# Four edits to the order of work in a two-layer hybrid encoder: latents scaled on ScalarE, key and value units inside gates, norm sums and pooled product one step later

## Chip, cores and metric

One core of one Trainium2 chip. The metric is the device time of one execution in microseconds. The profile names the engines PE (TensorE), DVE (VectorE), ACT (ScalarE), POOL (GpSimd) and SP (SyncE, which issues most DMAs).

## What is computed

The input is 512 tokens by 1024 features, float32. Each of two layers does this:

```python
h = rms_norm(x, attn_norm_g[l])
proj = h @ w_in[l]
c_q, c_kv, k_rope, gq, gk, gv, pool_in, gate_logits = split_columns(proj, IN_SIZES)
o_mla = mla_branch(c_q, c_kv, k_rope, ...)    # c_q, c_kv: RMS-normed, then up-projected to 8 heads
o_gqa = gqa_branch(gq, gk, gv, ...)           # 8 query heads, 2 key/value heads
o_pool = pool_branch(pool_in, ...)            # centred means over 2/4/8/16 tokens minus the token, a 128x128 map per group
gates = sigmoid(gate_logits)                  # three gates of 1024 features
merged = (gates[0] * (o_mla @ w_branch_mla[l]) + gates[1] * (o_gqa @ w_branch_gqa[l])
          + gates[2] * (o_pool @ w_branch_pool[l]))
x = x + merged @ w_out[l]
hf = rms_norm(x, ffn_norm_g[l])
u = depthwise_conv(hf @ ffn_w_up[l], ...)
x = x + (silu(u[..., :2816]) * u[..., 2816:]) @ ffn_w_down[l]
```

## The kernel before

**Arithmetic.** Every matmul operand is split into a high half, rounded to fp32r, and a low half, the remainder, and a product is three matmuls: high by high, high by low, low by high (`mm3`). The high half is an ACT copy, the low half a subtraction on DVE or POOL. Weights come from HBM in pieces of up to 512 columns, two or three to one DMA slot (tile `raw`, three buffers, read by SP). `w_split` makes `wh` on ACT and `wl` on POOL or DVE, three pieces ahead of use (`LA = 3`, six buffers). The next read into a `raw` buffer waits until the last `wl` of that buffer has been made.

**Order.** The order of instructions on every engine is written out when the kernel is built. `Clock` is a planner: each matmul moves its clock on by the number of columns over 2370 us, and the work of the other engines is queued as chains of steps that are issued when the planner thinks that their inputs are there. What is issued earlier stands earlier in an engine's queue, and each engine works in order. So a wrong guess of the planner makes an engine wait at the head of its queue. `ps(tag)` takes a bank of PSUM: `acc`, `ST` and `AV` have two banks, `S` and `mi` one.

**Stages of a layer.**

1. The latents `c_q` and `c_kv` (384 columns, token-major, four blocks of 128 tokens, banks acc and ST).
2. Pool channels, feature-major, four tiles of eight k-steps (three matmuls of 512 columns each). Between two k-steps `norm_finish` may issue the matmul that finishes the norm's sums (`prt`); `rt` and `rbc`, the row factors, follow from it. `norm_finish` is issued as soon as the planner thinks that `prt` is ready, at the latest at g == 1, n == 6. With `rt`, ACT evacuates the latents (`lat_evac`) and takes sums of squares; POOL raises them to the power -1/2 (`ssc`); DVE scales the four blocks by them (`lat_norm`), two instructions to a block. Then `lat_turn` transposes the blocks in 32x32 squares on DVE, writes them to HBM (`dl`, four writes) and reads them back feature-major (`tf`, twelve reads), all on SP, and splits them on ACT and DVE (`cth`, `ctl`).
3. GQA queries (512 columns, eight key steps, banks AV, AV, mi, ST). DVE rotates them (`gq_rope`), which frees the banks.
4. GQA keys, values and the rotary key (288 columns, eight key steps, banks acc, acc, S, ST). After four of these steps stands `pool_product`: four tiles in the banks of the queries, from the pooled channels `mixed` (`mxh`, `mxl`).
5. GQA attention, with gate and branch tiles as filler between its matmuls. A gate tile is eight units of one k-step, a branch tile four. `EXTRA` and `_order` put the up-projections of the MLA latents among them: four query units (`q`), two units of two blocks of keys without position (`n`), and two of values (`v`). All take the acc banks. A query unit stands before every second unit of the following tiles, a key or value unit before every fourth (`gap`): so the first stands before a gate, in the place between two tiles, and the second before its k-step 4. A value unit's bank is freed by two copies (`vm`, ACT or DVE) and four remainders on DVE.
6. Gate tiles alone, until the first MLA head is turned, and then MLA attention with the remaining gates and branches as filler.
7. The output projection, the second norm, the gated FFN with its convolution.

Of the kernel before, what the change touches and what calls it, by code (L numbers as in the profile page):

```python
# [14 lines left out]
ALU = mybir.AluOpType  # L15
# [3 lines left out]
P = 128  # L19
# [11 lines left out]
WIDE = 528  # L31
NWIDE = 5
RAW = 3
EXTRA = (("q", 2, (2, 5)), ("n", 2, (6, 7)), ("v", 1, (2, 5)))

SOONER = {1: 3 * KC, 0: 6 * KC}
LAG = {2: 1, 1: 4, 0: 8}
PRO = 0.47
PRE_A = 16
PRE_B = 8  # L40
LA = 3
# [4 lines left out]
        "mla": (-6.2, -2.9, -1.0, 0.1, 0.64, 1.678, 1.82, 35.5)}  # L46

D_ROW, D_OUT, D_IN, D_LAT = 3.4, 3.2, 4.0, 6.0
REST = 0.4
W_BIAS = 2.54  # L50
C_BIAS = 0.2
# [13 lines left out]
def _order(br):  # L65


    r, lag = [], LAG[br]
    for m in range(KC + lag):
        r += [(k, pos.index(m)) for k, b, pos in EXTRA if b == br and m in pos]  # L70
        if m < KC:
            r.append(("g", m))
        if m >= lag:
            r.append(("b", m - lag))
    return r
# [5 lines left out]

def _widths():

    r = [384] * KC + [T] * 8 + [T] * KC + [288] * 4 + [T] + [288] * 4
    for br in (2, 1, 0):
        for k, _ in _order(br):
            r += WIDTHS[k]
    return r + [T] * (2 * KC) + [T] * (4 * FC) + [T] * (2 * FC)


# [34 lines left out]
class Clock:  # L125
# [37 lines left out]
    def done(self, *key):  # L163
        self.ready[key] = self.fin + self.SEM
# [90 lines left out]
def trunk(ctx: ExitStack, tc: tile.TileContext, x, w, prm, gb, cst, out):  # L255
# [213 lines left out]

    def norm_finish(gen, out, force=False):  # L470

        if gen not in parts or not (force or ck.has(("prt", gen))):
            return
        need(("prt", gen))
        s2 = ps("S")
        mm(s2[:, :16], C[:, C_GRP:C_GRP + P], parts.pop(gen), True, True)
        a, a4 = small("fac", [P, 16]), small("fac4", [P, 16])
        rt, rbc = out["rt"], out["rbc"] = small("rt", [P, 4]), slot("rbc")

        def mean():  # L480
            V.tensor_scalar(a, s2[:, :16], 1.0 / D, EPS, ALU.mult, ALU.add)
            free("S")

        def tokens():
            V.tensor_tensor(a4, a, C[:, C_SEL:C_SEL + 16], ALU.mult)
            V.tensor_reduce(rt, a4.rearrange("p (b g) -> p b g", g=4), AX.X, ALU.add)
            done("rt", gen)

        def rows():
            V.transpose(rbc[:, :T].rearrange("p (j r) -> p j r", r=32), bc(a.unsqueeze(2), [P, 16, 32]))  # L490
            done("rbc", gen)

        chain(mean, lambda: G.tensor_tensor(a, a, bc(mhalf, [P, 16]), ALU.pow), tokens, rows, after=0.3)
# [43 lines left out]
    def layer(l, sq, xsrc):  # L537
# [36 lines left out]

        def tok_major(banks, wd, between=None):
            for kc in range(KC):
                if between and kc == 4:
                    between()
                wh, wl = wnext()
                need(("H", G1, kc))  # L580
                if st["use"] == 1:
                    for n, (x_, w_) in enumerate(((HH, wh), (HL, wh), (HH, wl))):
                        for b in range(4):
                            mm(banks[b][:, :wd], x_[:, kc, b * P:b * P + P], w_[:, :wd], n == 0, False)
                    continue
                for b in range(4):
                    bs = slice(b * P, b * P + P)
                    mm3(banks[b][:, :wd], HH[:, kc, bs], HL[:, kc, bs], wh[:, :wd], wl[:, :wd],
                        kc == 0, kc == KC - 1)
# [37 lines left out]
            for c0, n in ((0, 256), (1, 128)):  # L627
                V.tensor_scalar(ssc[:, :, c0:c0 + 1], ssc[:, :, c0:c0 + 1], 1.0 / n, EPS, ALU.mult, ALU.add)

        def lat_norm():  # L630
            for b in range(4):
                V.tensor_scalar(mx[b][:, 0:256], mx[b][:, 0:256], ssc[:, b, 0:1], None, ALU.mult)
                V.tensor_scalar(mx[b][:, 256:384], mx[b][:, 256:384], ssc[:, b, 1:2], None, ALU.mult)
            done("lat", l)

        def latents():
            chain(*[([("rt", G1)], lambda b=b: lat_evac(b)) for b in range(4)], lat_mean,
                  *rsqrt_steps(ssc.rearrange("p a b -> p (a b)"), 8, ("ssc", l)), lat_norm)

        latents()  # L640

# [46 lines left out]
        for g in range(4):  # L688
            acc = ps(ptags[g])
            for n, _ in enumerate(feat_major(acc, G1)):  # L690
                norm_finish(G1, nrm, g == 1 and n == 6)
            chain(*pool_steps(g, acc, ptags[g]))


# [2 lines left out]
        def lat_turn():  # L697
            d = dp.tile([4, P, 384], F32, tag=f"dl{l}", name=f"dl{l}")
            trs, tos = [], []

            def turn_block(b):
                trs.append(slot("tr"))
                V.transpose(trs[b][:, :384], mx[b][:, :384])

            def put(b):
                SY.dma_start(d[b], trs[b][:, :384])
                ck.fin = ck.now + (D_OUT if b == 3 else 0.1)

            def get(j):
                to = slot("tf")  # L710
                src = d.rearrange("b (i f) (c t) -> c f (b i) t", i=4, t=32)
                for c in range(4):
                    SY.dma_start(to[32 * c:32 * c + 32, :T].rearrange("f (g t) -> f g t", t=32), src[4 * j + c])  # L713
                chain(*split(lat[j][0][:, :T], lat[j][1][:, :T], to[:, :T], col(PRM_CQ + j)),
                      lambda: done("latT", l, j), after=D_LAT)
                ck.fin = ck.now + 1.5

            steps = []
            for b in range(4):
                steps += [lambda b=b: turn_block(b), lambda b=b: put(b)]  # L720
            chain(*steps, *[lambda j=j: get(j) for j in (2, 0, 1)], after=0.1)

        chain(([("lat", l)], lat_turn))


        qtags = ("AV", "AV", "mi", "ST")
# [140 lines left out]
        def gates(br, okey, odst, mode):  # L867
# [44 lines left out]
                    merged[m] = (mh, ml)  # L912
                    chain(product, add, *split(mh[:, :T], ml[:, :T], XM[:, m, :]), fin)

            extra, tick, gap = None, 0, 2
            for k, m in _order(br):
                if k in mla_make:
                    extra, tick, gap = mla_make[k](m), 0, 2 if k == "q" else 4
                    continue
                work = branch(m) if k == "b" else gate(m)  # L920
                more = True
                while more:
                    if extra and tick % gap == 0:
                        if next(extra, END) is END:
                            extra = None
                        yield
                    tick += 1
                    more = next(work, END) is not END
                    yield
# [675 lines left out]
def _pack_weights(i):  # L1605
    res = []
    for l in range(L):
        cq, ckv, kr, gq, gk, gv, pool, gate = np.split(
            i["w_in"][l], np.cumsum([256, 128, 32, 512, 128, 128, 512]), axis=1)

        def rows(*parts):
            wm = np.concatenate(parts, axis=1)
            return [wm[kc * P:kc * P + P] for kc in range(KC)]

        res += rows(cq, ckv)
        for g in range(4):
            res += _cut(_blocks(pool[:, g * P:g * P + P], KC))
        res += rows(gq)
        res += rows(gk, gv, kr)
        res.insert(len(res) - 4, i["pool_w"][l].transpose(1, 0, 2).reshape(P, T))  # L1620
        uq, ukv = i["mla_w_uq"][l], i["mla_w_ukv"][l].reshape(P, 8, P)

        wb = (i["w_branch_mla"][l], i["w_branch_gqa"][l], i["w_branch_pool"][l])
        for br in (2, 1, 0):
            for k, m in _order(br):
                c = slice(m * P, m * P + P)
                if k == "g":
                    res += _cut(_blocks(gate[:, br * D:(br + 1) * D][:, c], KC))
                elif k == "b":
                    res += _cut(_blocks(wb[br][:, c], 4))  # L1630
                elif k == "q":
                    res += [uq[kc * P:kc * P + P, m * 384:m * 384 + 384] for kc in range(2)]
                else:
                    c = slice(0, 64) if k == "n" else slice(64, P)
                    res.append(ukv[:, 4 * m:4 * m + 4, c].reshape(P, 256))
        for m in range(KC):
            res += _cut(_blocks(i["w_out"][l][:, m * P:m * P + P], KC))
        up = i["ffn_w_up"][l]
        for c in range(FC):
            for o in (0, D_FF):  # L1640
                res += _cut(_blocks(up[:, o + c * P:o + c * P + P], KC))
        dn = i["ffn_w_down"][l]
        res += _cut(np.concatenate([_blocks(dn[:, m * P:m * P + P], FC) for m in range(KC)], axis=1))
    pieces, swidth = _stream()
    assert [a.shape[1] for a in res] == [wd for _, _, wd in pieces]
    slots = [[] for _ in swidth]
    for (sl, _, _), a in zip(pieces, res):
        slots[sl].append(a)
    return np.concatenate([np.concatenate(a, axis=1).reshape(-1) for a in slots])
# [76 lines left out]
```

## Time and profile before

| | |
|---|---|
| median of 3 executions | 1580.51 us (1580.4 to 1582.9) |
| the profiled execution | 1580.47 us, of which 1578.5 us is the span of the profile |
| mean granted TensorE clock | 0.999 |
| busy: PE, DVE, ACT, POOL | 1566.6, 952.9, 787.4, 1021.1 us |
| instructions | 20363 |

In a profile row "start, duration, engine, line, operation, output <- inputs" the text in brackets is the idle time of the engine just before the instruction and what ended it; "xN" merges N instructions. Most operations are issued by a few helpers, so the tile tells more than the line. Matmuls overlap, and the shown duration of one is longer than its distance to the next.

### The profile page before, as it was taken

The numbers are of one execution on the slowest core, as the hardware profiler recorded it, in microseconds if no ns is written. First come the engines' busy times: TensorE is split into PE (matmuls) and PEld (weight loads), VectorE is DVE, ScalarE is ACT, GpSimd is POOL, SyncE is SP. The second block draws the span as 40 slices with busy tenths as digits, with TensorE's granted clock in tenths as the row PEclk, the third lists the DMA queues.
The fourth block names the chain that finished last, engine by engine and source line by source line (L and its number), as shares of the span: only waits on it lengthen the run. The fifth ranks groups of instructions, "written<-read, shape, count | busy, mean of one in ns | idle before, by whom it ended". The sixth has DMA issues, their size and how long they took to land.

```text
span 1578.5 us, 20363 instructions
## 1 busy us (share of the span) xinstructions
PE 1566.6 (99%) x7098; PEld 1310.3 (83%) x7098; DVE 952.9 (60%) x1360; ACT 787.4 (50%) x1426; POOL 1021.1 (65%) x890
## 2 busy tenths in 40 slices
PE   9999999999999999999999999999999999999999
PEld 8888888888888888888898888888888888888888
DVE  6877967866267776721047788678652777777000
ACT  6367866663444444432244677576534444444221
POOL 3864986854667667654577649868547766676542
PEclk9999999999999999999999999999999999999999
DMA  5432234314333233333334322343242223223331
GB/s 200 124 107 81 78 93 134 117 54 140 107 94 100 94 98 96 102 108 124 106 100 129 106 74 78 102 139 104 68 152 94 90 96 102 94 96 105 120 113 48
DMA packets 85927, 164.43 MB, mean 104 GB/s; under 512 B 25025, under 2 KB 47041, under 8 KB 85825
## 3 DMA queue, kind: packets, MB, share of 16 engines
q1 hardware_dynamic: 80928, 162.93, 33.3%
q8 instruction: 56, 0.92, 0.2%
q10 hardware_dynamic: 4896, 0.21, 0.2%
q14 instruction: 47, 0.38, 0.1%
HBM read 149.41 MB, written 13.63 MB: 103 GB/s over the span
## 4 chain that ended last, share of the span: by engine, by line
PE 87%; DVE 4%; POOL 2%; ACT 2%; issue 2%; DMA 2%; SPq 1%; POOLq 0%; ACTq 0%
PE ps_acc L367 39%; PE ps_AV L367 21%; PE ps_ST L367 21%; PE ps_S L367 3%; PE ps_mi L367 3%; DVE XM L223 1%; POOL wl L223 1%; DVE mgl L223 1%; ACT mgh L216 1%; POOL win L223 1%; SPq L713 1%; DVE gt L227 0%; DMA tf<-dtq 0%; ACT wh L216 0%; DMA tf<-dl 0%
## 5 line engine op out<-in xcount | busy, mean ns | idle before, releaser
L223 POOL TENSOR_TENSOR wl<-raw,wh 128x512 fp32r<-128x512 f32 (+2 forms) x503 | 674.2, 1352 | 413.3 <-ACT wh L216 374.4
L216 ACT ACTIVATE wh<-raw 128x512 fp32r<-128x512 f32 (+1 forms) x521 | 308.5, 607 | 124.8 <-PE ps_ST L367 42.0
L227 DVE SCALAR_TENSOR_TENSOR a<-u,prm,a 128x511 f32<-128x511 f32 x176 | 242.5, 1379 | 89.2 <-ACT a L216 84.3
L367 PE MATMUL ps_acc<-HH,wh 128*128 128x512 f32 x592 | 231.9, 392 | 0.5 <-DVE gt L223 0.5
L367 PE MATMUL ps_acc<-HH,wl 128*128 128x512 f32 x592 | 231.3, 391 | 0.0
L367 PE MATMUL ps_acc<-HL,wh 128*128 128x512 f32 x592 | 231.3, 391 | 0.0
L367 PEld LDWEIGHTS ps_acc<-HH,wl 128*128 128x128 f32 x592 | 111.3, 188 | 23.6
L367 PEld LDWEIGHTS ps_acc<-HH,wh 128*128 128x128 f32 x592 | 111.6, 188 | 23.0 <-issue 0.9
L367 PEld LDWEIGHTS ps_acc<-HL,wh 128*128 128x128 f32 x592 | 111.4, 188 | 22.9
L367 PE MATMUL ps_AV<-HH,wh 128*128 128x512 f32 x288 | 112.4, 390 | 0.0
L367 PE MATMUL ps_AV<-HH,wl 128*128 128x512 f32 x288 | 112.2, 390 | 0.0
L367 PE MATMUL ps_AV<-HL,wh 128*128 128x512 f32 x288 | 112.2, 390 | 0.0
L223 POOL TENSOR_TENSOR al<-a,ah 128x512 fp32r<-128x512 f32 x44 | 57.9, 1316 | 83.5 <-ACT ah L216 78.8
L231 DVE TENSOR_REDUCE nm<-ps_S 128x1 fp32r<-128x512 f32 x128 | 87.7, 685 | 37.5 <-PE ps_S L367 35.6
L367 PE MATMUL ps_ST<-HH,wh 128*128 128x512 f32 x240 | 93.7, 390 | 0.0
L367 PE MATMUL ps_ST<-HL,wh 128*128 128x512 f32 x240 | 93.5, 390 | 0.0
L367 PE MATMUL ps_ST<-HH,wl 128*128 128x512 f32 x240 | 93.5, 389 | 0.0
L216 ACT ACTIVATE ah<-a 128x512 fp32r<-128x512 f32 x44 | 27.8, 632 | 127.8 <-DVE a L223 127.8
L216 ACT ACTIVATE a<-u,prm 128x512 f32<-128x512 f32 x88 | 71.0, 809 | 27.0 <-DVE u L223 26.5
L216 ACT ACTIVATE a<-a 128x512 f32<-128x512 f32 x44 | 27.8, 632 | 106.2 <-DVE a L227 106.2
L216 ACT ACTIVATE HH<-XM,prm 128x512 fp32r<-128x512 f32 x32 | 23.1, 722 | 104.4 <-DVE XM L223 53.9
L216 ACT ACTIVATE ps_ST<-ps_ST 128x512 f32<-128x512 f32 x86 | 49.9, 581 | 39.8 <-PE ps_ST L367 38.0
(376 smaller groups left out, 3734.1 us busy)
## 6 DMA issues: line engine op xcount, KB each, us to landing
raw<-w SPq DMA_DIRECT2D x228, 512.0 KB, 3.5
raw<-w SPq DMA_DIRECT2D x13, 384.0 KB, 3.1
XM<-x SPq DMA_DIRECT2D x16, 256.0 KB, 4.2
dtq<-tr SPq DMA_DIRECT2D x16, 192.0 KB, 3.9
dtk<-tr SPq DMA_DIRECT2D x16, 192.0 KB, 4.0
tf<-dtq SPq DMA_DIRECT2D x48, 64.0 KB, 2.1
tf<-dtk SPq DMA_DIRECT2D x48, 64.0 KB, 2.4
raw<-w SPq DMA_DIRECT2D x6, 448.0 KB, 3.4
```

Source lines behind the costliest of these rows:

```text
L216: return self.eng.activation(out, in_, func, **k)
L223: return self.eng.tensor_tensor(out, *a)
L227: return self.eng.scalar_tensor_tensor(out, *a)
L231: return self.eng.tensor_reduce(out, in_, *a, **k)
L367: PE.matmul(o, lhsT=lhsT, rhs=rhs, start=start, stop=stop)
L713: SY.dma_start(to[32 * c:32 * c + 32, :T].rearrange("f (g t) -> f g t", t=32), src[4 * j + c])
```

## The change

- `lat_norm` becomes a step for each block of 128 tokens on ACT (a copy scaled by `ssc`, in place), and each block is turned as soon as it is scaled.
- A value unit stands before k-step 3 of a gate, one in each of two gates that follow each other; key units stand before k-steps 2 and 6 of a gate. The value units are moved forward, from before gates 2 and 5 of the GQA branch to gates 1 and 3. The packed weights follow this order.
- `norm_finish` is issued when the planner's clock is 2.0 us past the time at which it thinks that `prt` is ready.
- `pool_product` stands after five key steps instead of four.

```diff
-EXTRA = (("q", 2, (2, 5)), ("n", 2, (6, 7)), ("v", 1, (2, 5)))
+EXTRA = (("q", 2, (2, 5)), ("n", 2, (6, 7)), ("v", 1, (1, 3)))
+MID = 5
+D_SUM = 2.0
...
-        if gen not in parts or not (force or ck.has(("prt", gen))):
+        if gen not in parts or not (force or ck.ready.get(("prt", gen), 1e9) + D_SUM <= ck.now):
...
-                if between and kc == 4:
+                if between and kc == MID:
...
-        def lat_norm():
-            for b in range(4):
-                V.tensor_scalar(mx[b][:, 0:256], mx[b][:, 0:256], ssc[:, b, 0:1], None, ALU.mult)
-                V.tensor_scalar(mx[b][:, 256:384], mx[b][:, 256:384], ssc[:, b, 1:2], None, ALU.mult)
-            done("lat", l)
+        def lat_norm(b):
+            A.activation(mx[b][:, 0:256], mx[b][:, 0:256], AF.Copy, scale=ssc[:, b, 0:1])
+            A.activation(mx[b][:, 256:384], mx[b][:, 256:384], AF.Copy, scale=ssc[:, b, 1:2])
+            done("lat", l, b)
...
-                norm_finish(G1, nrm, g == 1 and n == 6)
+                norm_finish(G1, nrm, g == 1 and n == 7)
...
-                steps += [lambda b=b: turn_block(b), lambda b=b: put(b)]
+                steps += [([("lat", l, b)], lambda b=b: turn_block(b)), lambda b=b: put(b)]
...
-            extra, tick, gap = None, 0, 2
+            extra, tick, when = None, 0, None
...
-                more = True
+                more, first = True, tick
                 while more:
-                    if extra and tick % gap == 0:
+                    n = tick - first
+                    if extra and (tick % 2 == 0 if when == "q" else k == "g" and n in ((2, 6) if when == "n" else (3,))):
                         if next(extra, END) is END:
```

More of the change, by code (lines that the diff above doesn't have):

```diff
@@ L82, in _widths @@
 def _widths():
-    r = [384] * KC + [T] * 8 + [T] * KC + [288] * 4 + [T] + [288] * 4
+    r = [384] * KC + [T] * 8 + [T] * KC + [288] * MID + [T] + [288] * (KC - MID)
     for br in (2, 1, 0):
+        late = []
         for k, _ in _order(br):
-            r += WIDTHS[k]
+            if k in "nv":
+                late = WIDTHS[k]
+            else:
+                r += WIDTHS[k][:1] + late + WIDTHS[k][1:]
+                late = []
     return r + [T] * (2 * KC) + [T] * (4 * FC) + [T] * (2 * FC)
@@ L628, in lat_mean @@
                 V.tensor_scalar(ssc[:, :, c0:c0 + 1], ssc[:, :, c0:c0 + 1], 1.0 / n, EPS, ALU.mult, ALU.add)
-        def lat_norm():
-            for b in range(4):
-                V.tensor_scalar(mx[b][:, 0:256], mx[b][:, 0:256], ssc[:, b, 0:1], None, ALU.mult)
-                V.tensor_scalar(mx[b][:, 256:384], mx[b][:, 256:384], ssc[:, b, 1:2], None, ALU.mult)
-            done("lat", l)
+        def lat_norm(b):
+            A.activation(mx[b][:, 0:256], mx[b][:, 0:256], AF.Copy, scale=ssc[:, b, 0:1])
+            A.activation(mx[b][:, 256:384], mx[b][:, 256:384], AF.Copy, scale=ssc[:, b, 1:2])
+            done("lat", l, b)
         def latents():
             chain(*[([("rt", G1)], lambda b=b: lat_evac(b)) for b in range(4)], lat_mean,
-                  *rsqrt_steps(ssc.rearrange("p a b -> p (a b)"), 8, ("ssc", l)), lat_norm)
+                  *rsqrt_steps(ssc.rearrange("p a b -> p (a b)"), 8, ("ssc", l)),
+                  *[lambda b=b: lat_norm(b) for b in range(4)])
         latents()
@@ L719, in lat_turn @@
             for b in range(4):
-                steps += [lambda b=b: turn_block(b), lambda b=b: put(b)]
+                steps += [([("lat", l, b)], lambda b=b: turn_block(b)), lambda b=b: put(b)]
             chain(*steps, *[lambda j=j: get(j) for j in (2, 0, 1)], after=0.1)
-        chain(([("lat", l)], lat_turn))
+        chain(([("lat", l, 0)], lat_turn))
         qtags = ("AV", "AV", "mi", "ST")
@@ L913, in branch @@
                     chain(product, add, *split(mh[:, :T], ml[:, :T], XM[:, m, :]), fin)
-            extra, tick, gap = None, 0, 2
+            extra, tick, when = None, 0, None
             for k, m in _order(br):
                 if k in mla_make:
-                    extra, tick, gap = mla_make[k](m), 0, 2 if k == "q" else 4
+                    extra, tick, when = mla_make[k](m), 0, k
                     continue
                 work = branch(m) if k == "b" else gate(m)
-                more = True
+                more, first = True, tick
                 while more:
-                    if extra and tick % gap == 0:
+                    n = tick - first
+                    if extra and (tick % 2 == 0 if when == "q" else k == "g" and n in ((2, 6) if when == "n" else (3,))):
                         if next(extra, END) is END:
@@ L1619, in _pack_weights @@
         res += rows(gk, gv, kr)
-        res.insert(len(res) - 4, i["pool_w"][l].transpose(1, 0, 2).reshape(P, T))
+        res.insert(len(res) - KC + MID, i["pool_w"][l].transpose(1, 0, 2).reshape(P, T))
         uq, ukv = i["mla_w_uq"][l], i["mla_w_ukv"][l].reshape(P, 8, P)
         wb = (i["w_branch_mla"][l], i["w_branch_gqa"][l], i["w_branch_pool"][l])
+        late = []
         for br in (2, 1, 0):
@@ L1627, in _pack_weights @@
                 if k == "g":
-                    res += _cut(_blocks(gate[:, br * D:(br + 1) * D][:, c], KC))
+                    a, b = _cut(_blocks(gate[:, br * D:(br + 1) * D][:, c], KC))
+                    res += [a] + late + [b]
+                    late = []
                 elif k == "b":
@@ L1634, in _pack_weights @@
                     c = slice(0, 64) if k == "n" else slice(64, P)
-                    res.append(ukv[:, 4 * m:4 * m + 4, c].reshape(P, 256))
+                    late = [ukv[:, 4 * m:4 * m + 4, c].reshape(P, 256)]
         for m in range(KC):
```

## Prediction

> **What bounds the kernel now.** I read the head of the page first, then TensorE's own waits, then the places of those waits in the timeline, and last the engines that end them. Head of the page:
>
> ```profile
> span 1578.5 us, 20363 instructions
> PE 1566.6 (99%) x7098; PEld 1310.3 (83%) x7098; DVE 952.9 (60%) x1360; ACT 787.4 (50%) x1426; POOL 1021.1 (65%) x890
> ```
>
> TensorE is the bound: 11.9 us of its span are idle. The change adds and removes no matmul, so only TensorE's stalls can go or come. These waits are named (engine, tile, line, releaser: total, count, longest):
>
> ```profile
> PE ps_acc L367 <- DVE vm L223: 1.5, 2, 0.8
> PE ps_S L367 <- DVE prt L231: 1.3, 1, 1.3
> PE ps_mi L1561 <- DVE eps L251: 1.1, 1, 1.1
> PE ps_acc L367 <- POOL wl L223: 1.0, 2, 0.7
> PE ps_ST L367 <- ACT oph L216: 0.8, 1, 0.8
> PE ps_acc L367 <- ACT wh L216: 0.8, 1, 0.8
> PE ps_acc L367 <- DVE gt L223: 0.5, 2, 0.3
> ```
>
> All but the third lie where the change works. A busy span hides the restart after a wait, so I price each by starts: the distance between two matmuls, less the usual one. The usual one is 14.29/63 = 0.227 us for 512 columns (first row, from the chain) and 69.35 - 69.22 = 0.13 for 288 (timeline: start, duration, [idle before, releaser]).
>
> ```profile
> 222.01 14.29 PE ps_acc L367 x63
> 26.37 0.39 PE L367 MATMUL ps_AV<-HH,wl 128*128 128x512 f32 x1
> 28.03 0.40 PE L367 MATMUL ps_S<-prt,C 128*128 128x16 f32 x2 [1.27 <-DVE prt L231]
> 69.22 0.29 PE L367 MATMUL ps_ST<-wl,HH 128*128 128x288 f32 x1
> 69.35 0.30 PE L367 MATMUL ps_ST<-wh,HL 128*128 128x288 f32 x1
> 70.42 0.40 PE L367 MATMUL ps_acc<-wh,HH 128*128 128x288 f32 x1 [0.77 <-ACT wh L216]
> 71.52 0.40 PE L367 MATMUL ps_acc<-wl,HH 128*128 128x288 f32 x1 [0.71 <-POOL wl L223]
> 854.48 0.29 PE L367 MATMUL ps_acc<-wh,HH 128*128 128x288 f32 x1
> 855.07 0.40 PE L367 MATMUL ps_acc<-wl,HH 128*128 128x288 f32 x1 [0.30 <-POOL wl L223]
> 861.63 0.39 PE L367 MATMUL ps_mi<-mxh,wl 128*128 128x512 f32 x1
> 862.83 0.47 PE L367 MATMUL ps_ST<-mxh,wh 128*128 128x512 f32 x1 [0.81 <-ACT oph L216]
> 213.28 0.47 PE L367 MATMUL ps_acc<-HH,wh 128*128 128x512 f32 x1 [0.27 <-DVE gt L223]
> 244.60 0.39 PE L367 MATMUL ps_acc<-HH,wl 128*128 128x512 f32 x1
> 245.82 0.47 PE L367 MATMUL ps_acc<-oh,wh 128*128 128x512 f32 x1 [0.83 <-DVE vm L223]
> ```
>
> The stall at 70 us has a tail. By stretches (length, busy, PEclk, DMA):
>
> ```profile
> 69.30:73.00 3.70, 2.23 (x15) 0.98 0.07 26
> 73.00:76.40 3.40, 3.40 (x16) 0.52 0.71 224
> ```
>
> For 3.4 us the granted clock was about half: 3.40 x (1 - 0.52) = 1.63 us lost while "busy".
>
> **Part 1, norm sums.** Now the sum matmul is issued after six k-steps of the first pool tile and waits 28.03 - 26.37 - 0.23 = 1.43 us. The new condition asks for 2.0 us more on the planner's clock, where a k-step counts 3 x 512/2370 = 0.65: three or four k-steps. (The forced call at n == 7 can never happen, because the generator yields only n = 0 to 6; the clock alone decides.) Three k-steps on the chip are 9 x 0.227 = 2.04 us, over the 1.43. The wait goes, **-1.4**. What hangs on the sums (row factors, latents, pool evacuations) comes at most 2.7 - 1.4 = 1.3 us later in absolute time; the sums are first used by ACT and DVE, and TensorE needs no bank from them before the GQA queries, 26 k-steps or 17.7 us on. Layer 1 has no such wait. For the FFN norm the factors come about 2 us later, covered by six banks of 24 x 0.227 = 5.4 us each; if that cover were gone it would cost 2 us per layer.
>
> **Part 2, latents on ACT.** Eight scalings per layer leave DVE and go to ACT (DVE, layers 0 and 1; then two ACT operations of the same tile and widths):
>
> ```profile
> 46.33 6.66 DVE L235 TENSOR_SCALAR mx<-mx,ssc 128x256 f32<-128x256 f32 x8
> 825.83 3.99 DVE L235 TENSOR_SCALAR mx<-mx,ssc 128x256 f32<-128x256 f32 x8 [0.53 <-POOL ssc L223]
> 33.75 0.42 ACT L216 ACTIVATE junk<-mx 128x256 f32<-128x256 f32 x1
> 34.16 0.29 ACT L216 ACTIVATE junk<-mx 128x128 f32<-128x128 f32 x1
> ```
>
> On ACT: 4 x (0.42 + 0.29) = 2.84 us per layer, 3.8 and 1.2 us shorter than on DVE, and block 0 can be turned after 0.7 us. [...]
>
> ACT works in order, so weight halves (wh) stand behind a scaling that waits for POOL's power. ACT then has room:
>
> ```profile
> 58.61 0.63 ACT L216 ACTIVATE mxh<-win 128x512 fp32r<-128x512 f32 x1 [10.32 <-DVE win L227]
> 60.27 6.19 SPq L713 DMA_DIRECT2D tf<-dl  x12
> 69.31 0.72 ACT L216 ACTIVATE cth<-tf,prm 128x512 fp32r<-128x512 f32 x1 [2.05 <-DMA tf<-dl]
> 69.94 1.09 ACT L216 ACTIVATE wh<-raw 128x288 fp32r<-128x288 f32 x3
> ```
>
> If that room is not where the planner thinks, the cost is a wh wait like those at 70 us (about 2 us and 1.6 of clock). These rows also tell where the stall at 70 us comes from: twelve reads of the transposed latents leave SP at 60.27 to 66.46, the last lands before 69.31, ACT stands in front of it 2.05 us, and the next weight half begins only at 69.94. TensorE wants it at 69.48. An earlier scaling moves the four writes and twelve reads on SP with it. They are mixed with weight reads in that queue, and a weight read may hold them, or they it. In layer 0 the sums shift costs 0.6 to 1.3 us of the 3.8, DVE's freed 6.66 us let the pool windows and POOL's wl run earlier too; I take 3 us or more. The stall needs only 0.94 + 0.97 us. Layer 0: 70.42 - 69.35 - 0.13 = 0.94, 71.52 - 70.42 - 0.13 = 0.97, and 1.63 of clock: **-3.5**. Layer 1: 855.07 - 854.48 - 0.13 = **-0.5**. Bounds: 4.0 gained if all goes, 0 if SP holds the reads, 3.6 lost if ACT's room is not there.
>
> [...]
>
> **Part 3, pool product.** It runs after five key steps instead of four, 12 x 0.13 = 1.57 us later. In layer 1 its fourth tile waits 862.83 - 861.63 - 0.23 = 0.97 us. The profile names ACT, but oph is no input of it; the bank is, freed by the GQA rotation on DVE:
>
> ```profile
> 862.01 0.68 DVE L223 TENSOR_TENSOR gqr<-ps_ST,tabg 128x512 f32<-128x512 f32 x1
> ```
>
> This ends at 862.69, just ahead of 862.83. TensorE comes 0.5 us sooner and the product 1.57 later, so 1.1 later in all, which covers 0.97: **-1.0**. Bounds 0 to 1.0. In layer 0, where nothing waits now, the product comes 3.5 - 1.6 = 1.9 us sooner; this is late next if the rotation does not come sooner as well, and costs up to 1.9. The rotation hangs on ACT squares that stand behind the same 2.05 us wait, so I take it along. The product's results come 1.6 us later to the first branch tile, which has 16 gate units (16 x 0.68 = 10.9 us) in front.
>
> **Part 4, units inside gates.** Value units now stand before k-step 3 of a gate, one per gate; key units before k-steps 2 and 6. Both gate waits on "gt" (a value unit between two gates: the second gate wants the bank of the first at once) go: 2 x 0.27 = **-0.5**. The waits on "vm" are 245.82 - 244.60 - 0.23 = 0.99, and by the wait list 1.5 - 0.83 = 0.67 idle in layer 1: **-1.7** together if the bank is free in time. It has five units (3.4 us) instead of four (2.7), and the units of v(1) now lie before the MLA attention, no longer behind this:
>
> ```profile
> 242.58 0.72 ACT L216 ACTIVATE tf<-tf,gcol 96x512 f32<-96x512 f32 x1 [3.70 <-DMA tf<-dtq]
> 244.39 0.36 ACT L216 ACTIVATE vm<-ps_acc 128x256 fp32r<-128x256 f32 x1
> 244.79 0.89 DVE L223 TENSOR_TENSOR vm<-ps_acc,vm 128x252 fp32r<-128x252 f32 x4 [2.32 <-ACT vm L216]
> 228.83 0.63 ACT L216 ACTIVATE oh<-oraw 128x512 fp32r<-128x512 f32 x1 [2.96 <-DVE oraw L223]
> L367 PE MATMUL ps_acc<-wh,cth 128*128 128x384 f32 (+1 forms) x48 | 15.3, 319 | 0.0
> ```
>
> Query units already run two k-steps apart inside a gate, and with the key units between tiles they wait 0.0 us in the last row (groups by line). So a key unit two k-steps before a gate's end should cost nothing; if its copy is late, it costs what a gt wait costs, 0.27.
>
> **The sum.** 1.4 + 3.5 + 0.5 + 1.0 + 0.5 + 1.7 = 8.6 us if all goes and nothing comes. Unknown are waits that come elsewhere, since the planner re-orders four in-order queues and SP. The waits here are 0.3 to 1.4 us each, nine of them; I put back 2.0, two or three of that size. The profiled execution took 1580.47 us (span 1578.5), the median of three is 1580.51, so no correction: 1580.5 - 8.6 + 2.0 = **1573.9 us**. Own range 1571 to 1577.
>
> **Rivals.**
>
> 1. The latents come no sooner: SP's weight reads hold the writes, or ACT is not the faster engine in this place, its scalings standing behind weight halves for as long as they save. Then part 2 gives nothing, the rest stays: 1580.5 - 4.6 + 2.0 = 1577.9. For it: SP's reads of weights wait for POOL in the same queue. Against: the 6.66 us, and POOL runs freer without them. [...]
>
> 2. Everything goes, but as much comes back in the MLA attentions, whose order shifts by two units: a weight read on SP that waits for a late wl holds a head's reads behind it, and the scores and sums after them wait. With four such waits of 1 us per layer, 1580.5 - 8.6 + 8 = 1579.9. For it stands a wait that is there already:
>
> ```profile
> 315.27 0.62 PE L367 MATMUL ps_S<-kh,qa 96*128 96x512 f32 x1 [0.39 <-DVE nm L231]
> ```
>
> Against it: of its kind the list of waits has only this one.
>
> 3. Slower. The place is the stretch of gates between the attentions (222 to 236 us), where no attention matmul stretches the units and a bank must be free in 3.4 us. If the copy of a value unit falls in ACT's order behind both the wait for "oraw" (2.96) and a turned head (3.70), it is free after 2.96 + 3.70 + 0.36 + 0.9 (four DVE remainders) = 7.9 us (last rows of part 4), 4.5 too late, and the clock drops (1.63): 6.1 us a layer, 12.3 in all. Without part 4's "vm" gain the others save 6.9: 1580.5 + 12.3 - 6.9 = 1585.9. It decides once such a copy is held more than 3.4 us. Against: the second unit comes 14 units in, 9.5 us after 222, behind "oh".
>
> **How the numbers follow.** Forecast 0.68, rival 1 0.12, rival 2 0.09, rival 3 0.11. About 0.2% (3.2 us) is what a measurement can tell from no change. Faster by more (below 1577.3): forecast, 0.68. Within: rivals 1 and 2, with a little of the others, 0.20. Slower by more: 0.12 with smaller mishaps of the same kind. The low end, 1570.0, takes all 8.6 us and a chance wait or two of the attentions besides; the high end, 1581.0, takes in rivals 1 and 2 and leaves out rival 3.
>
> **What would show it.** The wait on "prt" gone, its matmul near 28.6 to 29.3 us; "mx" on ACT, eight in about 3 us; the twelve latent reads leaving SP several us sooner; PEclk 1.00 throughout 66 to 80 us; no "vm" or "gt" wait. Wrong would be: half clock again in the second product, waits on wh or wl there, or a "vm" wait of over 1 us between the attentions.

## The result: slower, and the profile after

The changed kernel takes 1586.01 us (median of 7; 1583.95 to 1587.69), the kernel before 1580.51 in the same comparison: ratio 1.0032 [1.0021, 1.0043], 5.5 us more. The profiled execution took 1585.94 us, 1584.1 of it span, with a granted clock of 0.997 (0.999 before). Head of the page of the changed kernel:

```profile
span 1584.1 us, 20341 instructions
PE 1567.5 (99%) x7098; PEld 1310.2 (83%) x7098; DVE 949.1 (60%) x1351; ACT 789.7 (50%) x1436; POOL 1022.0 (65%) x889
```

The span grew by 5.6 us and TensorE's busy time by 0.9 only: TensorE idles 16.6 us, not 11.9. These are its waits in the changed kernel (engine, tile, line, releaser: total, count, longest):

```profile
PE ps_acc L375 <- DVE vm L231: 5.7, 2, 2.9
PE ps_AV L375 <- DVE ssr L231: 4.2, 1, 4.2
...
PE ps_AV L375 <- ACT gkn L224: 0.5, 1, 0.5
```

The waits on "prt", "oph", "gt" and on POOL for "wl" are gone from the list and the one on "wh" is down to 0.3, so the forecast waits did go. "vm" did not go, it grew from 1.5 to 5.7 us, and a wait of 4.2 us for a bank AV is new.

The steps that came as forecast, in the timeline of the changed kernel (start, duration, engine, line, operation, [idle before, releaser]):

```profile
28.74 0.39 PE L375 MATMUL ps_AV<-HH,wl 128*128 128x512 f32 x1
29.18 0.40 PE L375 MATMUL ps_S<-prt,C 128*128 128x16 f32 x2
46.51 2.17 ACT L224 ACTIVATE mx<-mx,ssc 128x256 f32<-128x256 f32 x6
49.11 0.79 ACT L224 ACTIVATE mx<-mx,ssc 128x256 f32<-128x256 f32 x2
57.21 4.04 SPq L721 DMA_DIRECT2D tf<-dl  x8
62.16 2.03 SPq L721 DMA_DIRECT2D tf<-dl  x4
```

The matmul of the sums stands at 29.18 and waits 29.18 - 28.74 - 0.23 = 0.21 us; eight scalings take 2.96 us on ACT; the reads of the latents leave SP from 57.21 to 64.19, 2 to 3 us sooner. And what the change brought, by stretches of the changed kernel (length, busy time of each engine, PEclk, DMA share, GB/s):

```profile
66.00:80.00 14.00, 14.00 (x96) 13.30 (x95) 13.27 (x23) 9.93 (x20) 12.28 (x13) 1.00 0.41 122
82.48:85.89 3.41, 0.02 (x1) 0.00 (x0) 3.24 (x7) 3.35 (x13) 2.67 (x3) 1.00 0.63 194
85.89:92.72 6.83, 6.01 (x14) 4.80 (x15) 6.80 (x20) 0.34 (x1) 1.93 (x2) 0.50 0.11 44
229.25:232.67 3.42, 2.25 (x10) 1.51 (x9) 1.60 (x2) 1.09 (x4) 3.31 (x6) 1.00 0.00 0
232.67:236.08 3.41, 1.71 (x8) 1.44 (x9) 3.41 (x9) 0.63 (x1) 1.97 (x4) 1.00 0.46 140
1014.32:1017.73 3.41, 0.54 (x3) 0.22 (x2) 3.41 (x7) 0.00 (x0) 3.41 (x6) 1.00 0.05 10
1017.73:1021.14 3.41, 3.41 (x9) 2.63 (x9) 2.40 (x5) 0.63 (x1) 0.07 (x2) 0.50 0.93 265
```

The old stall at 70 us is away (14.00 busy of 14.00, clock 1.00). Instead TensorE stands still from 82.5 to 86.7 us, and the granted clock is half from 85.89 to 92.72 us; TensorE works 6.01 us of that (6.01 x 0.50 = 3.0 us lost; the matmuls of 512 columns start 0.43 us apart there, from 88.13 to 92.39, instead of 0.227). Between the attentions it stands 2.9 us, without half clock behind, and after the same wait in layer 1 the clock is half for 3.41 us (3.41 x 0.50 = 1.7 lost).

**The wait at 82 us.** The gate tile that opens the GQA stage needs bank AV. That bank holds a tile of the pooled product until DVE has taken its low half (`opl`). First the kernel before (DVE, and POOL beside it), then the changed kernel:

```profile
78.98 2.56 POOL L223 TENSOR_TENSOR gqr<-gqr,rp 128x512 f32<-128x512 f32 x2
80.26 0.74 DVE L227 SCALAR_TENSOR_TENSOR opl<-ps_AV,prm,oph 128x512 fp32r<-128x512 f32 x1
80.92 0.66 DVE L235 TENSOR_SCALAR y<-ssr 128x32 int32<-128x32 int32 x1
```

```profile
77.00 0.71 DVE L243 TENSOR_SCALAR y<-ssr 128x32 int32<-128x32 int32 x1
77.75 1.22 DVE L231 TENSOR_TENSOR yt<-y,ssr 128x32 f32<-128x32 f32 x1
78.89 5.00 POOL L231 TENSOR_TENSOR wl<-raw,wh 128x512 fp32r<-128x512 f32 x4
82.20 0.30 PE L375 MATMUL ps_ST<-wh,HL 128*128 128x288 f32 x1
83.97 0.19 DVE L235 SCALAR_TENSOR_TENSOR y<-yt,y 128x32 f32<-128x32 f32 x1
84.65 1.25 DVE L235 SCALAR_TENSOR_TENSOR ssr<-yt,y 128x32 f32<-128x32 f32 x1
85.82 0.74 DVE L235 SCALAR_TENSOR_TENSOR opl<-ps_AV,prm,oph 128x512 fp32r<-128x512 f32 x1
86.71 0.77 PE L375 MATMUL ps_AV<-HH,wh 128*128 128x512 f32 x1 [4.21 <-DVE ssr L231]
```

Between 77.00 and 85.82 the changed kernel's DVE works through the ten steps of the GQA query norm's inverse root, which `rsqrt_steps` hands over as one block. Before, one `opl` stood ahead of that block and freed the bank that the first gate tile takes. Now the product comes one key step later in TensorE's order (1.57 us), the planner puts the block first, and all four `opl` stand behind it. The profile names `ssr` as what ended the wait; that is the small step next to `opl` on DVE, and the gate tile does not read it. By starts the wait costs 86.71 - 82.20 - 0.13 = 4.4 us, and the half clock follows.

**The waits for "vm" between the attentions.** First the kernel before, then the changed kernel:

```profile
221.10 1.04 POOL L223 TENSOR_TENSOR MK<-MK,ssm 128x512 f32<-128x512 f32 x1
225.22 1.09 POOL L251 MEMSET osum<- 1x512 f32 x2
226.34 0.69 DVE L223 TENSOR_TENSOR oraw<-oraw,osum 128x512 f32<-128x512 f32 x1 [2.08 <-POOL osum L251]
```

```profile
228.11 0.66 ACT L224 ACTIVATE vm<-ps_acc 128x256 fp32r<-128x256 f32 x2 [0.69 <-PE ps_acc L375]
228.97 1.04 POOL L231 TENSOR_TENSOR MK<-MK,ssm 128x512 f32<-128x512 f32 x1
229.95 1.09 POOL L259 MEMSET osum<- 1x512 f32 x2
231.07 0.69 DVE L231 TENSOR_TENSOR oraw<-oraw,osum 128x512 f32<-128x512 f32 x1 [4.87 <-POOL osum L259]
231.11 0.39 PE L375 MATMUL ps_acc<-HH,wl 128*128 128x512 f32 x1
231.68 1.75 DVE L231 TENSOR_TENSOR wl<-raw,wh 128x512 fp32r<-128x512 f32 x1
233.35 0.87 DVE L231 TENSOR_TENSOR vm<-ps_acc,vm 128x252 fp32r<-128x252 f32 x4
234.37 0.47 PE L375 MATMUL ps_acc<-HH,wh 128*128 128x512 f32 x1 [2.87 <-DVE vm L231]
```

ACT copies the value unit in time (228.77). The four remainders that free its bank come at 233.35, since DVE stands 4.87 us at the head of its queue, for POOL to clear the sums of the last GQA head pair, and then makes a weight's low half (1.75 us). POOL clears the sums at 229.95 (225.22 before), behind the last step of a key norm (228.97, before 221.10): the key units run later, and the norm of the keys with them. That is only a part of the growth from 2.08 to 4.87 us: experiment 6, with the key units still inside the gates and the value units back at gates 2 and 5, has 3.02 us there. In the kernel before, no value unit stood behind DVE's wait. It costs 234.37 - 231.11 - 0.23 = 3.0 us, twice.

**The balance.** Gone: 1.2 (prt), 3.5 and 0.5 (70 us and its like in layer 1), 1.0 (product in layer 1), 0.5 (gt), 1.7 (old vm) = 8.4. Come: 4.4 + 3.0, 0.5 (AV in layer 1), 2 x 3.0 + 1.7, 0.3 (a wait for XM) = 15.9. That makes 7.5 more; 5.5 was measured. About 1 us of the rest lies in MLA waits of layer 0 near 315 us that are not there any more (by the starts of the matmuls there); their going was not isolated, and the rest is open.

### The profile page after: what moved, and what is told of

Same layout as the page of the kernel before. It is cut to its first block, busy times and chain, and to the rows that moved or that the text cites. A ratio compares the mean times of both kernels' runs of the same rounds, so it can differ in the third digit from the quotient of the medians.

```text
span 1584.1 us, 20341 instructions
## 1 busy us (share of the span) xinstructions
PE 1567.5 (99%) x7098; PEld 1310.2 (83%) x7098; DVE 949.1 (60%) x1351; ACT 789.7 (50%) x1436; POOL 1022.0 (65%) x889
## 4 chain that ended last, share of the span: by engine, by line
PE 90%; DVE 4%; POOL 2%; DMA 1%; ACT 1%; issue 1%; SPq 0%; ACTq 0%; POOLq 0%; DVEq 0%
PE ps_acc L375 40%; PE ps_AV L375 22%; PE ps_ST L375 21%; PE ps_S L375 3%; PE ps_mi L375 3%; DVE XM L231 1%; DMA raw<-w 1%; POOL wl L231 1%; DVE mgl L231 1%; ACT mgh L224 1%; DVE gt L235 0%; POOL win L231 0%; POOL tabm L231 0%; POOL fac L231 0%; DMA tf<-dl 0%
## 5 line engine op out<-in xcount | busy, mean ns | idle before, releaser
L224 ACT ACTIVATE wh<-raw 128x512 fp32r<-128x512 f32 (+3 forms) x521 | 308.8, 606 | 124.5 <-PE ps_ST L375 45.5
```

Of the source, the lines that this page charges most:

```text
L224: return self.eng.activation(out, in_, func, **k)
```

## The experiments

"Own before" is the kernel before in the same comparison (1580.03, 1579.82 and 1580.35 us in the three that follow).

**1. The product after four steps again.**

```diff
-MID = 5
+MID = 4
```

> The changed kernel with one edit undone: the pooled product again after four key steps instead of five. Theory A (order on DVE): one step later, the first remainder of the product (opl from bank AV) stands behind the ten small steps of the GQA query norm on DVE instead of ahead of them, so the first gate tile waits 4.2 us for bank AV at 82 us and the clock halves after it. Then that wait (4.4 us by starts), its slow clock (about 2.6) and layer 1's 0.5 us wait at the same place go; the fourth product tile may again wait up to 0.8 us for bank ST in each layer. 1586.0 - 7.7 + 1 = 1579. Rival (DVE is late there for other reasons, the latents moved to ACT or the norm sums): the wait only shifts by the 1.57 us of a step, at least 2.5 us of it and the slow clock stay, 1583 or more.

1580.68 us, ratio 1.0002 [0.9993, 1.0011]. The waits for vm stay at 5.7 us in all. Further down the list:

```profile
PE ps_ST L375 <- ACT oph L224: 0.7, 1, 0.7
```

The AV wait is gone and the product's own wait is back: the product's place makes the wait at 82 us. The time is 1.7 us above the 1579 expected. In the profiled execution the clock is half from 228.10 to 231.51 us (mean 0.76 in 225:231 and 0.92 in 231:234), behind the vm wait of layer 0, which no half clock follows in the changed kernel: 3.41 x 0.50 = 1.7 us.

**2. The clear of the sums of an attention's last head pair on DVE**, so that DVE no longer waits for POOL there.

```diff
-G.memset(sums[j:j + 1, :T], 0.0)
+(V if h == 7 else G).memset(sums[j:j + 1, :T], 0.0)
```

> The changed kernel; the two memsets of osum for the last head of an attention are issued on DVE instead of POOL. Theory A (DVE stands at the head of its queue): in the stretch between the attentions DVE waits 4.87 us for POOL's memset of osum, which stands behind the late key norms (MK) on POOL, and the remainders of the value unit (vm), behind that wait, free the bank 2.9 us late. Without the wait on POOL the remainders are done about 5 us sooner: both vm waits of 2.9 us fall under 0.5, layer 1's half clock after it (1.7) goes too: 1586.0 - 7.4 + 0.5 = 1579. Rival (the unit simply comes too early for DVE, with its own work of some 4 us in front): vm waits of 1.5 us or more each stay, 1583 or more.

1577.61 us, ratio 0.9985 [0.9975, 0.9995], 8.4 us below the changed kernel. No vm wait is left in the list:

```profile
PE ps_AV L375 <- DVE ssr L231: 6.5, 2, 4.2
```

The order of the units is untouched, so the wait for vm was DVE standing for POOL's clear. The AV wait grew in layer 1 to 2.3 us. There DVE and POOL show, in this kernel:

```profile
858.11 3.35 DVE L235 SCALAR_TENSOR_TENSOR ssr<-ssr,eps 128x32 f32<-128x32 f32 x1
858.09 1.30 POOL L231 TENSOR_TENSOR gqr<-gqr,rp 128x512 f32<-128x512 f32 x1
859.35 0.82 POOL L231 TENSOR_TENSOR wl<-raw,wh 128x288 fp32r<-128x288 f32 x1
860.12 1.29 POOL L231 TENSOR_TENSOR gqr<-gqr,rp 128x512 f32<-128x512 f32 x1
```

An instruction on 32 columns holds DVE for 3.35 us, from the start of the first of three POOL instructions to the end of the last.

**3. Key and value units between the tiles again** (order, places and packing of the weights as before; the other three edits stay).

```diff
-EXTRA = (("q", 2, (2, 5)), ("n", 2, (6, 7)), ("v", 1, (1, 3)))
+EXTRA = (("q", 2, (2, 5)), ("n", 2, (6, 7)), ("v", 1, (2, 5)))
...
-if extra and (tick % 2 == 0 if when == "q" else k == "g" and n in ((2, 6) if when == "n" else (3,))):
+if extra and tick % gap == 0:
```

> The changed kernel with the key and value units back where they were (value units before gates 2 and 5, units before every fourth k-step, weights packed as before); latents, norm sums and product as changed. Both theories of the vm wait have it gone at 231 and 1014 us (-2.9 - 2.9 - 1.9 of restarts and clock), with the old gt and vm waits back (0.3 to 1.0 us, four, about 2.8): 1586.0 - 7.7 + 2.8 = 1581. The wait at 82 us stays at about 4.2 us if it belongs to the product's place (theory A), and falls under 2 if the units have a part in it (rival).

1582.46 us, ratio 1.002 [1.0009, 1.0032].

```profile
PE ps_AV L370 <- DVE ssr L226: 6.4, 2, 4.4
...
PE ps_acc L370 <- DVE vm L226: 1.1, 2, 0.6
```

The vm wait falls to 1.1, gt comes back with 0.5, the AV wait stays. The two new waits have separate causes.

**4. The query norm on POOL**: only the first guess of the inverse root stays on DVE, its three refinements run on POOL, and the block goes as four pieces instead of one.

```diff
-*rsqrt_steps(ssr[:, 0:32], 32, ("ssr", l))
+*rsqrt_steps(ssr[:, 0:32], 32, ("ssr", l), G)
```

> The changed kernel, product after five steps; the Newton steps of the GQA query norm run on POOL instead of DVE. Theory A: the remainders of the product no longer stand behind ten DVE steps of up to 1.2 us, bank AV is free some 8 us sooner, the 4.2 us wait at 82 us and its slow clock go (-7.2): 1579, unless the queries' norm comes so late on POOL that the GQA attention begins later (each us of that would show as gate units before the attention, not as a wait). Rival (the product is late because its step is 1.57 us later and ACT's part comes later): the wait stays over 2.5 us.

1577.38 us, ratio 0.9981 [0.9972, 0.9991], 8.6 below the changed kernel, with the product still after five steps. Its longest waits are the two for vm, 5.7 us in all as in the changed kernel. No AV wait is left in either layer, and the four `opl` run from 77.14 to 79.85. So it was the block ahead of them on DVE. Whether shorter pieces on DVE would have done as well wasn't tried.

**5. Both queue edits (2 and 4) on the changed kernel.**

> The changed kernel with both queues cleared: the clear of the sums for the second head of a pair on DVE and the query norm's ten steps on POOL. If the two waits are independent, the gains add: 1586.0 - 8.4 (clear on DVE alone, 1577.6) - 8.6 (query norm on POOL alone, 1577.4) = 1569.0 us, with both the AV wait near 82 us and the two vm waits of 2.9 us gone and no stretch of half clock in layer 0 between 80 and 235 us. Rival: one gain is partly only time moved, because the later tiles then find their weights or buffers late; then 1572 to 1576 us, with new waits on weight pieces or on XM.

1569.98 us, ratio 0.9939 [0.9924, 0.9953]: 9.8 us below the kernel before, the fastest of all, level with experiment 10 (1570.28). The two gains add, within a microsecond. The whole list of its waits:

```profile
PE ps_mi L1570 <- DVE eps L259: 1.1, 1, 1.1
PE ps_acc L375 <- DVE mgl L231: 0.5, 2, 0.2
PE ps_S L375 <- DVE prt L239: 0.2, 1, 0.2
```

**6. The value units at gates 2 and 5 again, still inside the gate.**

```diff
-("v", 1, (1, 3))
+("v", 1, (2, 5))
```

> The changed kernel with the value units back at places 2 and 5 of the gates between the attentions, still inside the gate. Theory that the value unit overtakes the clear of the sums behind the key norms: the wait of 2.9 us for vm goes below 0.7 in each layer and the time falls by 6.1 us and the half clock of layer 1 (1.7), to about 1578 to 1580 us; the AV wait at 82 us stays at 4.2. Rival, that the key units' later start makes everything behind them late wherever the value unit stands: a wait of 2 us or more for vm or for the first attention tile stays in each layer, and the time stays above 1582 us.

1583.35 us, ratio 1.0019 [1.001, 1.0028]. Its waits, and DVE between the attentions (timeline):

```profile
PE ps_AV L375 <- DVE ssr L231: 6.2, 2, 4.2
...
PE ps_acc L375 <- DVE vm L231: 0.9, 2, 0.4
```

```profile
229.07 0.69 DVE L231 TENSOR_TENSOR oraw<-oraw,osum 128x512 f32<-128x512 f32 x1 [3.02 <-POOL osum L259]
230.02 0.87 DVE L231 TENSOR_TENSOR vm<-ps_acc,vm 128x252 fp32r<-128x252 f32 x4
```

The vm wait is 0.4 per layer, but not because the value unit gets past DVE's wait: its remainders stand behind it here too. DVE waits 3.02 us instead of 4.87, and the remainders follow 0.95 us after the wait instead of 2.28, with no weight's low half between. Experiment 3, with key and value units back, has 2.08 us there, as the kernel before. So the key units lengthen DVE's wait by 0.9 us and the value units' place by 1.9 more; through which of POOL's steps the second comes was not isolated. The time is 3 us or more above what I expected: the AV wait in layer 1 is 2.0 us here with half clock from 872.20 to 875.62 behind it (mean 0.57 in 872:876), where the changed kernel had 0.5 and none (1.00 in 866:880). That this wait varies between kernels with the same product place goes with POOL's timing (the 3.35 us row above); it was not tried by itself.

**7 and 8. The kernel before with the latents on ACT alone, and with the norm sums as well.**

> The kernel before with only the latents' scaling moved from DVE to ACT, block by block. If that alone takes away the stall near 70 us with its half clock (3.5 us) and layer 1's 0.97 us: 1580.0 - 4.5 = 1575.5 us, and no wait for rt near 70 us. Rival, that the stall in the kernel before also needed the norm sums' wait ahead of it to go: a wait of 1 us or more stays at that place, 1578 to 1580 us. The pooled product stands in its old place, so that the wait for AV at 82 us is not there in either case.

> The kernel before with the latents on ACT and the norm sums' matmul one step further back, without the moves of the product and of the units. If the forecast's first two parts hold, 1.4 us below the kernel with the latents alone: about 1574 us, with the prt wait at 0.1 or less. Rival: the wait for the sums hides another for the same bank or the same engine, and the difference of the two kernels is under 0.5 us.

1576.71 us, ratio 0.9982 [0.9973, 0.9991], and 1575.78 us, ratio 0.9974 [0.9965, 0.9984]. The longest wait and two stretches of the first of them:

```profile
PE ps_acc L367 <- DVE vm L223: 1.9, 2, 1.2
```

```profile
69.30:73.00 3.70, 3.70 (x30) 3.70 (x30) 3.70 (x9) 3.14 (x7) 3.70 (x4) 1.00 0.39 123
73.00:76.40 3.40, 3.07 (x17) 2.34 (x15) 3.40 (x9) 1.67 (x3) 3.40 (x5) 1.00 0.38 143
```

The latents alone remove the stall at 70 us and its half clock: 3.1 us of the 4.0 forecast, since the vm wait grows by 0.4 and another for "nm" by 0.3. The product's wait in layer 1 goes too, but one of 0.8 us comes at the product in layer 0 (76.87 us): with the stall gone the product is early there, as part 3 had warned. The sums bring 0.9 more, of 1.4; the intervals of the two ratios overlap, so the times alone do not settle this, but the prt wait is gone from the list.

**9 to 11. With both queue edits: the product after four steps, the units between the tiles, and both.**

> The changed kernel with both queues cleared (1570.0 us), and the pooled product after four row blocks again. If the product's move is worth what the forecast's part 3 said once its remainders have a free queue, this is 1.0 us slower, 1571.0 us, with a wait of 0.7 for bank ST at the product. Rival, that the move is worth nothing even then: 1570.0 within 0.4 us.

> The changed kernel with both queues cleared (1570.0 us), and the units of latent keys and values between the tiles again as in the kernel before. If the units' move is worth the forecast's part 4 (0.5 for gt, 1.7 for vm) once the clear of the sums doesn't wait on POOL, this is 2.2 us slower, 1572.2 us, with waits for gt and vm of that size. Rival, that the clear on DVE already takes the vm wait away by itself: only the 0.5 for gt comes back, 1570.5 us.

> The changed kernel with both queues cleared, and without both moves: the kernel before with latents on ACT, sums one step back and the two queue edits. If the moves add up as the forecast had them: 1570.0 + 1.0 + 2.2 = 1573.2 us. Rival, that the queue edits carry all of the gain over the 1575.8 us of latents and sums together: 1570.0 to 1570.6 us.

1574.16 us, ratio 0.9958 [0.9945, 0.997]; 1570.28 us, ratio 0.9936 [0.9922, 0.9949]; 1574.49 us, ratio 0.9963 [0.9951, 0.9976]. Together with the runs above they make two squares; each number is the time less its own before:

| | neither move | units moved | product moved | both |
|---|---|---|---|---|
| DVE's queue as changed | -4.0 | +0.7 | +2.4 | +5.5 |
| both queue edits | -5.9 | -6.2 | -10.1 | -9.8 |

As the change has the queues, the product's move costs 6.4 and 4.8 us and the units' move 4.7 and 3.1 (the last is the least sure: the intervals of the two kernels, [1.0009, 1.0032] and [1.0021, 1.0043], overlap). With the two edits the product's move gains 4.2 and 3.6 us, and the units' move is worth nothing within the spread (-0.3 and +0.3). So the 2.2 us that I gave the units are not theirs: with the clear on DVE the old vm wait is nearly away without them (the list of "neither" has none). The product's move is worth more than the 1.0 forecast. The waits of "product after four" that go with the move:

```profile
PE ps_ST L375 <- DVE gqr L231: 0.7, 1, 0.7
PE ps_mi L375 <- DMA qa<-nm: 0.7, 1, 0.7
PE ps_S L375 <- DVE nm L239: 0.6, 1, 0.6
```

The first is the product's own. The other two lie in the MLA attentions, far behind the product; why an earlier product brings them was not isolated.

**12. The kernel before with the two queue edits alone.**

> The kernel before with the two queue edits alone (clear of the second sums on DVE, query norm on POOL). If they only take away waits that the change made, the time is that of the kernel before, 1580 us, within 1 us, with the stall near 70 us in place. Rival, that they take the old vm and gt waits away too: 1577.5 to 1578.5 us.

1579.26 us, ratio 0.9991 [0.9982, 0.9999]: 1.1 us. The old vm wait shrinks from 1.5 to 0.2 in it, but others come (XM 0.7, gqr 0.6). So the edits are hardly a gain of their own, they remove what the two moves had made: they are worth 15.3 and 12.5 us where the product has moved, 6.9 where only the units have, 1.9 on latents and sums alone.

## Why the prediction was wrong

I forecast 1573.9 us, and 1586.0 came. What goes was read well, what comes was not.

- **Part 1** held: the matmul at 29.18, its wait 0.21 us instead of 1.43; by itself 0.9 us measured against 1.4, not clear of the spread.
- **Part 2** held: both stalls went with the latents alone; 3.1 us against 4.0. The rows for the ACT scalings (2.84 us for eight) came true, 2.96 us. But ACT is not the faster engine for one scaling, as the prediction read its rows. One by one, nine of DVE's sixteen took 0.27 to 0.34 us and seven 1.07 to 1.40, and ACT's took 0.38 to 0.50. In layer 0 the five long ones lie beside five POOL instructions of 1.09 to 1.29 us that follow each other from 46.28 to 52.18, the three short ones in POOL's pause behind them. So what the move to ACT saves is the 0.8 to 1.1 us by which a scaling on DVE was longer beside POOL, not the scaling itself.
- **Part 3** is the step that failed first. "The product's results come 1.6 us later to the first branch tile, which has 16 gate units [...] in front" names the wrong user. The results' first user is far off, but the banks' next user is the gate tile itself, and a bank comes free only with `opl`. I looked at who reads the result and not at who takes the bank, nor at what DVE's order puts ahead of `opl`. What stands there is a block of ten, handed over in one piece.
- **Part 4** failed in its cover: "It has five units (3.4 us) instead of four". I priced ACT's copy, and the copy is in time. The remainders on DVE stand behind a 4.87 us wait for POOL's clear, which I left out. That wait was 2.08 in the kernel before; 0.9 of its growth comes with the key units, whose norm stands ahead of the clear on POOL, and 1.9 with the value units' new place (experiments 3 and 6). I counted key units as costing nothing, by their own waits, and left out what their norm pushes back. The forecast 0.5 for gt came; the 1.7 for vm turned into 6.0 and half clock.
- **The 2.0 us put back for new waits** was mis-sized: 15.9 came. It was sized by the waits of the kernel before, 0.3 to 1.4 us each. The large ones, 4.4 and 3.0, came from what stood ahead in DVE's queue, and the clock's loss (3.0 behind the first, 1.7 behind the one in layer 1) came on top.
- **Rival 3** had the place (222 to 236 us), the condition (a unit's bank held over 3.4 us) and by chance the time, 1585.9. Its queue was wrong: it named ACT, experiment 2 shows DVE behind POOL. Its 12.3 us for this place measured 8.4 (experiment 2 takes that away), and nearly as much came from the AV wait that no rival had. Rivals 1 and 2 fell: the latents did come sooner, and the waits in the MLA attentions became fewer.

The chance of 0.12 for slower was too low: three of the four edits move work past queues on which other engines wait, and I had followed one queue for each.

## What to carry to other kernels

When a step is moved later, list the buffers that it holds and who takes them next, not only who reads its results, and follow the instruction that frees each buffer through its own queue: what stands ahead of it there, and what that waits for. A move that loses may only need its freeing instruction to get past one block: here two edits of one line, worth 1.1 us alone, turned +5.5 us into -9.8. Test the moves of a bundle in a square, with and without the obstacle, before a part is thrown out.

## What the hardware showed that I had not expected

**DVE's small steps took as long as POOL's instruction beside them.** In the changed kernel a step on 128x32 takes 1.22 us while POOL makes a `wl` (5.00/4 = 1.25 us each), 0.19 in POOL's pause at 83.97, 1.25 when POOL works again at 84.65 (rows of the wait at 82 us), and 3.35 us under three POOL instructions in layer 1 of experiment 2. `opl`, which reads PSUM, takes 0.74 us beside POOL's `gqr` (80.26 in the kernel before) and 0.73 without POOL work (87.91 in the changed kernel). What ties the small steps to POOL's instructions was not isolated. The block of ten is 8.8 us long (77.00 to 85.82), where ten steps of 0.19 would be about 2, by my estimate.

**Of two equal waits one had half clock behind it.** In the changed kernel the wait of 2.88 us in layer 1 is followed by half clock (0.50 in 1017.73:1021.14), the wait of 2.87 us in layer 0 is not (1.00 in 232.67:236.08). So a wait of this length cost 1.7 us more in one place and nothing more in the other. In the traces of the two kernels half clock lasts 6.83 us from 85.89, 3.41 from 1017.73, and 3.41 from 72.88 in the kernel before. My estimate from these numbers is that the place of a wait makes the difference: the 925.01 us at full clock from 92.72 to 1017.73 are 271 times 3.4133, and counted in such steps the wait in layer 1 lies whole in one, 1014.32 to 1017.73, while the one in layer 0 is cut at 232.67 into 1.17 and 1.71 us (3.42 - 2.25 and 3.41 - 1.71 in the rows of the stretches). No run shifted a wait to test it. The idle time in a step does not decide alone: the stall at 70 us in the kernel before had less in its step than 1.71, 3.41 - 1.94 = 1.47 us, and half clock followed:

```profile
69.47:72.88 3.41, 1.94 (x13) 1.55 (x12) 2.14 (x5) 3.41 (x8) 2.44 (x3) 1.00 0.03 11
72.88:76.29 3.41, 3.41 (x16) 3.41 (x15) 3.41 (x9) 1.97 (x5) 3.41 (x5) 0.50 0.68 213
```

In experiment 3 the times go with the clock: of its seven executions three had a mean granted clock of 0.997 and took 1583.8 to 1586.6 us, three had 0.998 and took 1580.5 to 1582.5, and one had 0.999 and took 1579.9. The four of experiment 5, whose longest wait is 1.1 us, had 1.000 and lie within 0.4 us.
